# Scan of a two-layer diffusion block: bonus values from the steps' own tiles, the merged inverse evicted where it is made, the state evicted behind the output products

## Chip, cores and metric

One Trainium2 chip, one of its cores. A core has five engines that run side by side, each through its own list of instructions in order: TensorE (PE, whose weight loads the profile lists apart as PEld), VectorE (DVE), ScalarE (ACT), GpSimd (POOL) and SyncE (SP). Data comes from device memory by DMAs, which SP issues in its order, and POOL for the fill's inputs. The metric is the device time of one execution in microseconds (us), as the median of some runs; lower is better.

## What is computed

Layer 0 mixes tokens with a recurrence, layer 1 with long convolutions, and behind each stands a dense MLP. The change concerns the recurrence of layer 0 and its readout. The sequence has 256 latent tokens and 256 context tokens, 2048 channels, 32 heads of 64.

```python
def step(S, inp):
    w_t, k_t, v_t, kk_t, b_t = inp[:5]
    S = (S * w_t[:, :, None, :]
         - jnp.einsum('bhvk,bhk->bhv', S, kk_t)[..., None] * b_t[:, :, None, :]
         + v_t[..., None] * k_t[:, :, None, :])
    out = jnp.einsum('bhvk,bhk->bhv', S, inp[5]) if emit else None
    return S, out
...
S_f, oc_f = wkv_scan(S0, rc, decc[0], kdc[0], vc, kkc, bc[0], False)
S_b, oc_b = wkv_scan(S0, rc, decc[1], kdc[1], vc, kkc, bc[1], True)
_, o_f = wkv_scan(S_f, r, dec[0], kd[0], v, kk, b[0], False)
_, o_b = wkv_scan(S_b, r, dec[1], kd[1], v, kk, b[1], True)
...
# readout of o = o_f + o_b: GroupNorm by head, bonus, gate, projection
o = ((o - mean) * lax.rsqrt(var + LNX_EPS)).reshape(B, L, D) * lnx_w + lnx_b
bonus = jnp.sum(r[None] * kd * r_k, axis=(0, -1))[..., None] * v
g = jax.nn.sigmoid((h + xx * mu[5]) @ g1) @ g2
return ((o + bonus.reshape(B, L, D)).astype(h.dtype) * g) @ w_o
```

Each direction is scanned over the context first, for its state alone, and from that state over the latent tokens, with outputs.

## The kernel before

**Chunks and groups.** The recurrence is not run token by token. Tokens are taken in chunks of 64, and within a chunk everything becomes products of 64x64 matrices: a triangular system is inverted once, and a step then makes four kinds of products with its inverse, the values and the state. The 32 heads are done in eight groups of four: two pairs of heads (`pi`), each pair on 128 partitions with one head to each half of 64 (`hs`). Both directions (`d`) run at once. A group has eight steps (`i`): steps 0 to 3 are the four context chunks (`st` 0), steps 4 to 7 the four latent chunks (`st` 1, with outputs).

**One step** (`scan_step`) has three parts, between which other work is put, so that PE has something to do while another engine evicts what it made:

- j=0: products of the values `VU` with `N` and of the decayed inputs with the state `Z`, into the PSUM tile `pr`; ACT evicts the sum to `rhs`.
- j=1: products of the inverse `Y` (tile yf in the profile) with `rhs`, into the other half of `pr`, and of the state with the decay, into the first writes of `po`; ACT evicts the former, negated, to the half of `VU` that holds no values. In a step with outputs, products of the state with the queries too.
- j=2: products of `KR` with the whole of `VU` give the new state, in half 1 of `po`; ACT evicts it as `Z`. In a step with outputs, products of `VU` with `KR` (sc<-KR,VU in the profile) add to half 0 of `po`, and ACT or DVE put them into `OT`. Both halves of `po` lie in one PSUM bank.

**What is put between.** `rwkv_scan` writes the order out by hand. In each third n = 3 i + j of a step it emits, in this order: the step's own part; at j=0 the matrices of the next step (`scan_products`: three PSUM tiles of the pool sg, evicted as NT and KR); at j=1 the loads of the next step's values (`scan_values`, four DMAs); so many pieces of the next group's preparation as `SCHED[n]` says; at j=1 one piece of the modulation's product (`ada`); in the thirds of `READ` one piece of the previous group's readout; and at j=1 and j=2 three pieces of a fill: the projection of the values of the next group (`fill_v`) or of the queries of the one behind it (`fill_r`), 18 products of 128x256 a time (fl in the profile), whose inputs fx POOL loads into three buffers. In the eighth group there is nothing to prepare, and the filters of layer 1 take the fill's place.

While `self.pins` is set, each instruction of PE, ACT and DVE depends on the one before it on its engine, so that the scheduler keeps this order. DMAs are free.

**The pool sg** has three buffers of one bank, taken in turn by `scan_products`, the preparation's products, the readout's and the modulation's transposes. A product that takes a buffer waits until what was in it is evicted.

**Preparation** of a group (`scan_prepare`, 36 pieces): the decays, `KB` and `ard`; the matrices `Mn`; `scan_bonus`, which sums r*k*r_k over a head's channels and leaves the sum `bs` of a pair, 128x256, in SBUF; then 31 steps of substitution on DVE (tmp and d in the profile), which invert blocks of 32; two transposes on DVE; and the merge of the blocks: two product groups with `Mn` (sg<-d,Mn, line 1207), evicted to `G`, and one group with `G` (sg<-d,d, line 1221), made in the last third of the group. Its result `py` is evicted to `Y` by four copies of 32 partitions, two on DVE and two on ACT, a piece of its own (lines 1223 to 1226). `prep` carries this piece over: it is taken in the first third of the next group, ahead of `scan_products` (line 919).

**Readout** (`scan_readout`, lines 1293 to 1354) of a group runs in the thirds `READ` = 6, 7, 9 (first pair) and 13, 14, 16 (second pair) of the next group. In the first third it loads the gate `gt`, takes the mean and squares; in the second it takes the variance, scales by lnx_w, and then loads the latent values of the pair again (`values`, two DMAs of 64 KB in rows of 256 B, into the tile sqo that the squares have left); in the last third PE transposes the values by products with the identity (sg<-ident,sqo), DVE multiplies them by `bs`, adds, multiplies by the gate, and SP stores y. The last group's readout (`late`) does its loads in step 5, the rest at the end, both pairs side by side.

**Values** lie in device memory as `v` (group, 512 tokens, 256), with the columns of a group ordered pair, head, channel, so a chunk's load for one head of both pairs has rows of two times 64 numbers (256 B each).

Of the kernel before, what the change touches and what calls it, by code (L numbers as in the profile page):

```python
# [18 lines left out]
P = 128  # L19
# [49 lines left out]
class Kern:  # L69
# [802 lines left out]
    def rwkv_scan(self, es, prep_pools, ngroups=KT // 2):  # L872
# [88 lines left out]
    def scan_values(self, g, i):  # L961
# [12 lines left out]
    SCHED = (1, 1, 1, 2, 1, 2, 1, 1, 2, 1, 1, 2, 1, 2, 2, 1, 2, 2, 1, 2, 2, 1, 2, 1)  # L974
# [134 lines left out]
    def scan_bonus(self, pi, res):  # L1109
# [41 lines left out]
    def scan_prepare(self, g):  # L1151
# [70 lines left out]
        yield  # L1222
# [5 lines left out]
    def scan_step(self, g, i):  # L1228
# [12 lines left out]
        for pi, d, blk, c in blks:  # L1241
            for h, hp in enumerate(hs):
                self.product(pr[hp, 0, blk, :], N[hp, blk, :], VU[hp, pi, d, h, :], start=True, stop=not i)
# [22 lines left out]
        nc.scalar.mul(VU[hs[1], :, :, 0, :], v4(pr[hs[1], 1]), -1.0)  # L1266
        nc.scalar.mul(VU[hs[0], :, :, 1, :], v4(pr[hs[0], 1]), -1.0)
# [25 lines left out]
    def scan_readout(self, g):  # L1293
# [8 lines left out]
        src = scr["v"][g, L:, :].rearrange("(c s) (p h v) -> h s c p v", s=64, h=2, v=64)  # L1302

        def pair(pi):
            m = 2 * g + pi
            tile_ = lambda: (self.sc if last and pi else self.sg).tile([P, 512], F32, name="sc" if last and pi else "sg")
            gt = rp.tile([P, L], F32, name="gt", bufs=n)
            nc.sync.dma_start(gt, scr["gate"][m * P : (m + 1) * P, :])
            o = OT[:, pi, :]
            bs = res["bs", pi]  # L1310

            def values():
                V = rp.tile([P, L], F32, name="sqo", bufs=n)[:].rearrange("p (c v) -> p c v", v=64)
                for h in range(2):
                    nc.sync.dma_start(V[64 * h : 64 * h + 64], src[h][:, :, pi, :])
                yield
                pt = self.sg.tile([P, 512], F32, name="sg")
                for c in range(4):
                    for hp in self.HS:
                        self.product(pt[hp, c * 64 : c * 64 + 64], V[hp, c, :], self.ident[hp, hp], start=True, stop=True)  # L1320
                nc.vector.tensor_tensor(bs, pt[:, :L], bs, op=ALU.mult)

            if last:
                yield from values()
                yield
# [11 lines left out]
            if last:  # L1337
                yield
            else:
                yield from values()  # L1340
# [5 lines left out]
        if last:  # L1346
            its = [pair(0), pair(1)]
            for _ in range(5):
# [374 lines left out]
def layout(inp):  # L1723
# [11 lines left out]
        "w_r": g["rw_w_r"], "w_k": g["rw_w_k"], "w_v": g["rw_w_v"], "w_o": g["rw_w_o"],  # L1735
# [41 lines left out]
```

## Time and profile before

| | us |
|---|---|
| median of 3 runs | 3775.41 (3771.19 to 3782.73) |
| profiled execution | 3769.96 |
| its span | 3768.1 |
| the scan within it, from the first step to the last output | about 580 to 1516 |
| mean granted TensorE clock | 0.944 |
| busy: PE, DVE, ACT, POOL | 3402.8, 2513.1, 1741.7, 684.7 |

The profile gives times of one execution, on its one core. In its rows "a<-b,c" means that a tile named a is written from b and c; a line number is often a helper's (L110 is `product`, L53 the wrapper of ACT and DVE), so groups are told apart by tile names. "Idle before" is the time in which the engine stood still ahead of an instruction, and behind the arrow stands what ended it. [...] The names of two operands come in no fixed order. fp32 products are carried out as several instructions, so counts are multiples of those in the code.

### The profile page before, as it was taken

What the parts mean: (1) busy time and instruction counts of PE and PEld (TensorE: products, weight loads), DVE (VectorE), ACT (ScalarE), POOL (GpSimd) and SP (SyncE); (2) the same over time, 40 slices, a digit from 0 to 9 for tenths busy, and PEclk for the clock granted to TensorE, in tenths of its full rate; (3) what the DMA queues carried; (4) which work ended last, traced back from release to release, by engine and by line L of the source; (5) the groups of instructions that cost most, each with busy time, mean ns of one, the idle gap of its engine ahead of it and who ended that gap; (6) DMA issues with size and microseconds to landing.
All of it is one profiled execution on the core that took longest, in us unless ns stands there. A gap on an engine that the chain in (4) does not pass through costs nothing.

```text
span 3768.1 us, 82300 instructions
## 1 busy us (share of the span) xinstructions
PE 3402.8 (90%) x34206; PEld 3119.8 (83%) x34206; DVE 2513.1 (67%) x3857; ACT 1741.7 (46%) x3045; POOL 684.7 (18%) x706
## 2 busy tenths in 40 slices
PE   7798888888888879889999999899998899999997
PEld 3376677777777767889999999899998799999997
DVE  5887676556566665578776776677787674646554
ACT  4444444443344434444343435465665663534342
POOL 2632221111111100110000001524443730000003
PEclk9899999888888979999999999999999999999998
DMA  9678798887788754668888887566665675656553
GB/s 322 192 229 262 247 314 260 236 237 224 220 236 238 232 149 131 208 207 292 265 276 268 281 266 238 168 216 218 214 218 173 218 232 182 187 182 186 183 184 108
DMA packets 694367, 838.34 MB, mean 222 GB/s; under 512 B 81055, under 2 KB 562240, under 8 KB 693992
## 3 DMA queue, kind: packets, MB, share of 16 engines
q1 hardware_dynamic: 662888, 719.82, 61.1%
q0 software_dynamic: 31104, 113.26, 9.8%
q8 instruction: 268, 4.39, 0.5%
q14 instruction: 107, 0.88, 0.1%
HBM read 778.36 MB, written 54.59 MB: 221 GB/s over the span
## 4 chain that ended last, share of the span: by engine, by line
PE 43%; DMA 15%; DVE 10%; issue 9%; ACT 4%; POOL 3%; SPq 1%; POOLq 0%; ACTq 0%; DVEq 0%
PE mm L158 11%; PE mm L159 11%; PE mm L160 11%; DMA aw<-in_ada_w 7%; PE fl L110 3%; DMA w<-in_mlp_up 2%; DVE wl L53 2%; PE sg L110 2%; PE sc L110 2%; POOL acc L293 2%; DMA sqo<-v 2%; DVE acc L53 1%; DMA fx<-xv 1%; ACT wh L53 1%; ACT aw L53 1%
## 5 line engine op out<-in xcount | busy, mean ns | idle before, releaser
L53 DVE TENSOR_TENSOR wl<-w,wh 128x1024 fp32r<-128x1024 f32 (+1 forms) x716 | 925.4, 1296 | 552.9 <-ACT wh L53 542.4
L53 ACT CAST wh<-w 128x1024 fp32r<-128x1024 f32 (+1 forms) x716 | 741.4, 1044 | 775.7 <-PE mm L159 479.3
L158 PE MATMUL mm<-hxh,wh 128*128 128x258 f32 (+1 forms) x3072 | 873.2, 286 | 23.3 <-ACT hxh L53 18.1
L160 PE MATMUL mm<-hxh,wl 128*128 128x258 f32 (+1 forms) x3072 | 870.7, 285 | 8.7 <-DVE wl L53 8.6
L159 PE MATMUL mm<-hxl,wh 128*128 128x258 f32 (+1 forms) x3072 | 872.1, 284 | 0.2 <-DVE hxl L53 0.2
L158 PEld LDWEIGHTS mm<-hxh,wh 128*128 128x128 f32 x3072 | 582.6, 190 | 26.8 <-ACT hxh L53 19.0
L160 PEld LDWEIGHTS mm<-hxh,wl 128*128 128x128 f32 x3072 | 581.7, 190 | 13.2 <-DVE wl L53 11.6
L159 PEld LDWEIGHTS mm<-hxl,wh 128*128 128x128 f32 x3072 | 584.3, 190 | 3.2 <-DVE hxl L53 1.3
L159 PE MATMUL mm<-ul,wh 128*128 128x256 f32 x2048 | 579.2, 283 | 8.0 <-DVE ul L53 7.8
L158 PE MATMUL mm<-uh,wh 128*128 128x256 f32 x2048 | 578.4, 283 | 5.5 <-ACT uh L53 5.5
L160 PE MATMUL mm<-uh,wl 128*128 128x256 f32 x2048 | 577.9, 282 | 0.0
L293 POOL TENSOR_TENSOR acc<-acc,aw 128x512 f32<-128x512 f32 x180 | 276.5, 1536 | 895.0 <-ACT aw L53 853.1
L159 PEld LDWEIGHTS mm<-ul,wh 128*128 128x128 f32 x2048 | 391.2, 191 | 9.1 <-DVE ul L53 9.1
L158 PEld LDWEIGHTS mm<-uh,wh 128*128 128x128 f32 x2048 | 391.0, 191 | 6.0 <-ACT uh L53 5.9
L160 PEld LDWEIGHTS mm<-uh,wl 128*128 128x128 f32 x2048 | 391.6, 191 | 0.0
L53 DVE SCALAR_TENSOR_TENSOR acc<-aw,sc,acc 128x512 f32<-128x512 f32 x300 | 230.9, 770 | 105.9 <-DMA aw<-in_ada_w 103.3
L110 PE MATMUL fl<-fh,fx 128*128 128x256 f32 x1024 | 233.7, 315 | 21.7 <-DMA fx<-xv 19.9
L110 PEld LDWEIGHTS fl<-fh,fx 128*128 128x128 f32 x1024 | 184.9, 212 | 43.2 <-DMA fx<-xv 24.9
L53 ACT ACTIVATE aw<-aw,sc 128x512 f32<-128x512 f32 x180 | 126.1, 719 | 134.3 <-DMA aw<-in_ada_w 126.8
L53 DVE TENSOR_TENSOR flo<-fr,fh 128x512 fp32r<-128x512 f32 x128 | 87.7, 686 | 124.8 <-ACT fh L53 120.5
L751 POOL DMA_DIRECT2D fx<-xv x128 | 67.9, 530 | 534.4 <-PE fl L110 520.4
L110 PE MATMUL sg<-ard,KB 64*64 64x64 f32 (+1 forms) x3584 | 135.0, 249 | 32.9 <-ACT yf L53 26.0
(351 smaller groups left out, 6203.9 us busy)
## 6 DMA issues: line engine op xcount, KB each, us to landing
aw<-in_ada_w SPq DMA_DIRECT2D x288, 512.0 KB, 5.9
w<-in_mlp_down SPq DMA_DIRECT2D x128, 1024.0 KB, 5.5
w<-in_mlp_up SPq DMA_DIRECT2D x120, 1024.0 KB, 6.3
fx<-xv POOLq DMA_DIRECT2D x128, 512.0 KB, 6.3
aw<-in_ada_w SPq DMA_DIRECT2D x192, 256.0 KB, 3.0
w<-in_hy_in_w SPq DMA_DIRECT2D x44, 1024.0 KB, 5.8
fx<-xr POOLq DMA_DIRECT2D x64, 512.0 KB, 5.5
w<-in_w_k SPq DMA_DIRECT2D x16, 1024.0 KB, 7.8
```

Source lines behind the costliest of these rows:

```text
L53: return self.kern.pin(self.key, f(*a, **kw))
L110: return self.pin("pe", self.nc.tensor.matmul(out, lhsT=lhsT, rhs=rhs, **kw))
L158: nc.tensor.matmul(out, lhsT=wh, rhs=xh, start=first, stop=False)
L159: nc.tensor.matmul(out, lhsT=wh, rhs=xl, start=False, stop=False)
L160: nc.tensor.matmul(out, lhsT=wl, rhs=xh, start=False, stop=last)
L293: nc.gpsimd.tensor_tensor(acc, acc, w[:, a], op=ALU.add)
L751: self.nc.gpsimd.dma_start(x, src)
```

## The change

- `scan_prepare` loses the piece between the inverse's last products and its eviction; both are one piece now, the 35th, in the last third of the group. `prep` carries nothing over. `SCHED` has the same sum, with its entries for thirds 21, 22 and 23 changed from 1, 2, 1 to 2, 1, 1.
- The values' columns are ordered group, head, pair, channel: the host permutes the columns of `w_v`, and `VU` is laid out [direction, head, pair, 64]. A load of a chunk for one head takes rows of 128 numbers (512 B).
- The bonus is multiplied in the steps with outputs: at j=1, behind the state's products with the queries, four products with the identity transpose the values that `VU` holds for that chunk into a tile of sg, and DVE multiplies them into `bs`, which is one tile for both pairs.
- In a step with outputs the products into half 0 of `po` come ahead of the eviction of `Z`, not behind it.
- The readout loads no values. The gate is loaded in the second third, behind the scaling by lnx_w, into the tile sqo that the squares have left. In the last group the readout has three rounds, all at the end, and nothing in step 5.

```diff
-        prep = iter((None,))
...
-            prep = itertools.chain(prep, () if last else self.scan_prepare(g + 1))
+            prep = iter(()) if last else self.scan_prepare(g + 1)
...
-                take(prep, 1)
                 prep_pools.close()
...
-                            take(prep, i == 0 and not last)
                             for _ in nxt:
                                 pass
...
-                if i == 5 and last:
-                    pins, self.pins = self.pins, None
-                    take(late, 1)
-                    self.pins = pins
...
-            src = self.scr["v"][g, t0 : t0 + 64, :].rearrange("s (p h v) -> h s p v", h=2, v=64)
             for h, hp in enumerate(self.HS):
-                self.nc.sync.dma_start(VU[hp, :, d, h, :], src[h])
+                self.nc.sync.dma_start(VU[hp, d, h], self.scr["v"][g, t0 : t0 + 64, h * P : (h + 1) * P].rearrange("s (p v) -> s p v", v=64))
...
-    SCHED = (1, 1, 1, 2, 1, 2, 1, 1, 2, 1, 1, 2, 1, 2, 2, 1, 2, 2, 1, 2, 2, 1, 2, 1)
+    SCHED = (1, 1, 1, 2, 1, 2, 1, 1, 2, 1, 1, 2, 1, 2, 2, 1, 2, 2, 1, 2, 2, 2, 1, 1)
...
-        bs = self.ge.tile([P, L], F32, name="bs", bufs=5)
-        self.nc.scalar.copy(bs, pb[:, :L])
-        res["bs", pi] = bs
+        if not pi:
+            res["bs"] = self.ge.tile([P, 2, L], F32, name="bs", bufs=3)
+        self.nc.scalar.copy(res["bs"][:, pi, :], pb[:, :L])
...
-        yield
         for d in range(2):
             for h in range(2):
                 (nc.scalar.copy if h else nc.vector.tensor_copy)(Y[part(h, d), d, :, 32 - 32 * d : 64 - 32 * d], py[part(h, d)])
...
+            pt = self.sg.tile([P, 2, 64], F32, name="sg")
+            for pi in range(2):
+                for h, hp in enumerate(hs):
+                    self.product(pt[hp, pi, :], VU[hp, 0, h, pi, :], self.ident[hp, hp], start=True, stop=True)
+            bs = res["bs"][:, :, 64 * il : 64 * il + 64]
+            nc.vector.tensor_tensor(bs, bs, pt, op=ALU.mult)
         yield
         if i < 7:
             for pi, d, blk, c in blks:
                 for h in range(2):
-                    mm(h, 1, blk, KR[:, h, blk, 0, :], VU[:, pi, d, h, :])
+                    mm(h, 1, blk, KR[:, h, blk, 0, :], VU[:, d, h, pi, :])
+        if st == 1:
+            for pi, d, blk, c in blks:
+                for h in range(2):
+                    mm(h, 0, blk, VU[:, d, h, pi, :], KR[:, h, blk, 1, :])
+        if i < 7:
             Zn = cp.tile([P, 4, 64], F32, name="Z")
             nc.scalar.copy(Zn, po[:, 1])
             res["Z"] = Zn
         if st == 1:
-            for pi, d, blk, c in blks:
-                for h in range(2):
-                    mm(h, 0, blk, VU[:, pi, d, h, :], KR[:, h, blk, 1, :])
...
-            gt = rp.tile([P, L], F32, name="gt", bufs=n)
-            nc.sync.dma_start(gt, scr["gate"][m * P : (m + 1) * P, :])
...
-            def values():
-                V = rp.tile([P, L], F32, name="sqo", bufs=n)[:].rearrange("p (c v) -> p c v", v=64)
-                for h in range(2):
-                    nc.sync.dma_start(V[64 * h : 64 * h + 64], src[h][:, :, pi, :])
-                yield
...
-            if last:
-                yield
-            else:
-                yield from values()
+            gt = rp.tile([P, L], F32, name="sqo", bufs=n)
+            nc.sync.dma_start(gt, scr["gate"][m * P : (m + 1) * P, :])
+            yield
             nc.vector.scalar_tensor_tensor(dv, dv, self.col("lnx_b", m), bs, op0=ALU.add, op1=ALU.add)
             nc.vector.tensor_tensor(dv, dv, gt, op=ALU.mult)
             nc.sync.dma_start(scr["y"][m * P : (m + 1) * P, :], dv)
...
+        "w_v": g["rw_w_v"].reshape(1, D, 8, 2, 2, 64).swapaxes(3, 4).reshape(1, D, D), "w_o": g["rw_w_o"],
```

More of the change, by code (lines that the diff above doesn't have):

```diff
@@ L1242, in scan_step @@
             for h, hp in enumerate(hs):
-                self.product(pr[hp, 0, blk, :], N[hp, blk, :], VU[hp, pi, d, h, :], start=True, stop=not i)
+                self.product(pr[hp, 0, blk, :], N[hp, blk, :], VU[hp, d, h, pi, :], start=True, stop=not i)
             if i:
@@ L1265, in scan_step @@
         v4 = lambda t: t.rearrange("p (a d) v -> p a d v", d=2)
-        nc.scalar.mul(VU[hs[1], :, :, 0, :], v4(pr[hs[1], 1]), -1.0)
-        nc.scalar.mul(VU[hs[0], :, :, 1, :], v4(pr[hs[0], 1]), -1.0)
+        for h in range(2):
+            nc.scalar.mul(VU[hs[1 - h], :, h].rearrange("p d a v -> p a d v"), v4(pr[hs[1 - h], 1]), -1.0)
         if st == 1:
@@ L1275, in scan_step @@
                 for h in range(2):
-                    mm(h, 1, blk, KR[:, h, blk, 0, :], VU[:, pi, d, h, :])
+                    mm(h, 1, blk, KR[:, h, blk, 0, :], VU[:, d, h, pi, :])
+        if st == 1:
+            for pi, d, blk, c in blks:
+                for h in range(2):
+                    mm(h, 0, blk, VU[:, d, h, pi, :], KR[:, h, blk, 1, :])
+        if i < 7:
             Zn = cp.tile([P, 4, 64], F32, name="Z")
@@ L1301, in scan_readout @@
         rp = self.rp if last else gp
-        src = scr["v"][g, L:, :].rearrange("(c s) (p h v) -> h s c p v", s=64, h=2, v=64)
         def pair(pi):
@@ L1306, in pair @@
             tile_ = lambda: (self.sc if last and pi else self.sg).tile([P, 512], F32, name="sc" if last and pi else "sg")
-            gt = rp.tile([P, L], F32, name="gt", bufs=n)
-            nc.sync.dma_start(gt, scr["gate"][m * P : (m + 1) * P, :])
             o = OT[:, pi, :]
-            bs = res["bs", pi]
-            def values():
-                V = rp.tile([P, L], F32, name="sqo", bufs=n)[:].rearrange("p (c v) -> p c v", v=64)
-                for h in range(2):
-                    nc.sync.dma_start(V[64 * h : 64 * h + 64], src[h][:, :, pi, :])
-                yield
[L1317 to L1321, printed above, removed]
-            if last:
-                yield from values()
-                yield
+            bs = res["bs"][:, pi, :]
             ps = tile_()
@@ L1336, in pair @@
             nc.vector.scalar_tensor_tensor(dv, dv, self.col("lnx_w", m), sq, op0=ALU.mult, op1=ALU.mult)
-            if last:
-                yield
-            else:
-                yield from values()
+            gt = rp.tile([P, L], F32, name="sqo", bufs=n)
+            nc.sync.dma_start(gt, scr["gate"][m * P : (m + 1) * P, :])
+            yield
             nc.vector.scalar_tensor_tensor(dv, dv, self.col("lnx_b", m), bs, op0=ALU.add, op1=ALU.add)
@@ L1347, in scan_readout @@
             its = [pair(0), pair(1)]
-            for _ in range(5):
+            for _ in range(3):
                 for it in its:
@@ L1734, in layout @@
         "ada_w": g["ada_w"], "mlp_up": g["mlp_up"], "mlp_down": g["mlp_down"],
-        "w_r": g["rw_w_r"], "w_k": g["rw_w_k"], "w_v": g["rw_w_v"], "w_o": g["rw_w_o"],
+        "w_r": g["rw_w_r"], "w_k": g["rw_w_k"],
+        "w_v": g["rw_w_v"].reshape(1, D, 8, 2, 2, 64).swapaxes(3, 4).reshape(1, D, D), "w_o": g["rw_w_o"],
         "dec_w1": g["rw_dec_w1"], "dec_w2": g["rw_dec_w2"], "a_w1": g["rw_a1"], "a_w2": g["rw_a2"],
```

## The prediction

> **What bounds the kernel now.** The change touches the scan alone, from 580 to 1516 us of the span, so after the page's head I read the scan: its windows, PE's groups and waits there, and single stretches of the timeline.
>
> ```profile
> span 3768.1 us, 82300 instructions
> ```
>
> The windows of the scan (us; busy time of PE, PEld, DVE, ACT, POOL; granted clock, DMA share, GB/s), one of the eight groups of four heads, then the first seven together:
>
> ```profile
> 813.00:930.00 117.00, 97.79 (x1884) 86.48 (x1884) 72.05 (x154) 50.29 (x120) 13.85 (x27) 0.88 0.81 233
> 580.00:1380.00 800.00, 667.90 (x13079) 588.88 (x13078) 497.18 (x1065) 345.05 (x823) 90.68 (x171) 0.88 0.79 231
> ```
>
> A group takes about 117 us. PE is the busiest engine, yet idles 800 - 668 = 132 us of the 800, and its clock is 0.88. Both can be gained. Who ends PE's idle time, in groups of instructions (busy us, mean ns, idle before) and as waits (total, times, longest):
>
> ```profile
> L110 PE MATMUL fl<-fh,fx 128*128 128x256 f32 x896 | 204.3, 315 | 12.2 <-DMA fx<-xv 12.2
> L110 PE MATMUL sg<-ard,KB 64*64 64x64 f32 (+1 forms) x3184 | 117.5, 249 | 32.2 <-ACT yf L53 26.0 <-DVE NT L53 3.7 <-ACT KR L53 2.5
> L110 PE MATMUL sc<-KR,VU 128*64 128x64 f32 x448 | 20.4, 237 | 18.9 <-ACT Z L53 18.9
> L110 PE MATMUL sg<-d,Mn 32*32 32x32 f32 x896 | 19.1, 203 | 10.3 <-issue 8.1 <-DVE d L53 2.1
> L110 PE MATMUL sg<-ident,sqo 64*64 64x64 f32 x192 | 15.3, 291 | 40.1 <-DMA sqo<-v 31.8 <-DVE d L53 5.6 <-DVE tmp L53 2.8
> ```
>
> ```profile
> PE sg L110 <- DMA sqo<-v: 31.8, 15, 6.4
> PE sg L110 <- ACT yf L53: 26.0, 7, 4.2
> PE sc L110 <- ACT Z L53: 18.9, 21, 2.3
> ```
>
> PE waits 40.1 us for the readout's values, 26.0 for the merged inverse's eviction (3.7 a group) and 18.9 for the state's eviction: 85 of the 132 us, and the change goes at these three.
>
> **What a wait costs beyond itself** is seen in the clock, microsecond by microsecond (PE busy, clock, DMA share, GB/s), behind a wait for values:
>
> ```profile
> 846.00:847.00 1.00, 0.70 (x24) 1.00 1.19 319
> 847.00:848.00 1.00, 0.00 (x0) 1.00 1.21 259
> 848.00:849.00 1.00, 0.00 (x0) 0.68 1.10 243
> 849.00:850.00 1.00, 0.00 (x0) 0.50 0.73 182
> 850.00:851.00 1.00, 0.94 (x16) 0.50 0.14 40
> ...
> 855.00:856.00 1.00, 1.00 (x9) 0.91 0.35 71
> ```
>
> The clock halves while PE idles, some 2 us after its last product (846.7 to 848.7), and stays at 0.50 for 6.8 us (0.64 + 6 + 0.18). What that costs the fill's products:
>
> ```profile
> 882.60 0.41 PE L110 MATMUL fl<-flo,fx 128*128 128x256 f32 x1
> 882.81 0.63 PE L110 MATMUL fl<-fh,fx 128*128 128x256 f32 x2
> ...
> 888.26 0.28 PE L110 MATMUL fl<-fx,flo 128*128 128x256 f32 x1
> 888.38 0.40 PE L110 MATMUL fl<-fx,fh 128*128 128x256 f32 x2
> ```
>
> From one product's start to the next it is 0.21 us at half clock and 0.12 at full: 43% is lost. A clock of 0.88 over 800 us is 2 x 0.12 x 800 = 192 us at half, some 28 stretches of 6.8. In microsecond windows I count 17 of them right behind one of the first two waits (last below); PE is busy for some 5.7 us of a stretch, so one costs 2.5 us, and the 17 cost 43.
>
> ```profile
> 1312.00:1313.00 1.00, 0.00 (x0) 0.00 (x0) 0.00 (x0) 0.58 (x2) 0.00 (x0) 0.79 0.52 171
> ```
>
> Here the clock fell after 2 us without a product, so value waits of 31.8 / 15 = 2.1 us in the mean count too. [...]
>
> **The change, part by part.**
>
> **Bonus values in the steps.** Gone are the loads sqo<-v, the transposing products behind them and their wait: 40.1 us. The same 16 transposes a group now run as four bursts of four, reading tiles already loaded: no difference on PE. On DVE two products of 128x256 become four of 128x128.
>
> ```profile
> L53 DVE TENSOR_TENSOR bs<-sg,bs x16: 416/425/426, 731.4 to 1506.7; 128x256 f32<-128x256 f32 x16
> ```
>
> ```profile
> L53 DVE TENSOR_TENSOR OT<-OT,sc x32: 277/280/289, 662.4 to 1504.5; 128x128 f32<-128x128 f32 x32
> ```
>
> That is 4 x 0.28 - 2 x 0.425 = +0.3 us a group, on an engine that has 45 us of a group to spare. The burst adds a wait: it takes one of the three sg buffers, which only DVE's multiplication gives back, and the state's products and all fills stand behind it on PE. Nothing of before shows it; bounds are 0 and the 3.7 us that the inverse's eviction costs. Nearest is the wait for DVE's NT, behind like products: 3.7 us in seven groups, 0.5 each. I take 0.3.
>
> **The gate's load** moves behind the scaling by lnx_w, where the value loads stood on SP, so SP waits there as now, one load instead of three; its queue loses the early gate load and both value loads of each readout. Behind it wait only DVE's product with the gate and the store of y; before, DVE stood there for PE anyway. Its landing (3.1 us against 5.9, below) should come first.
>
> **Merged inverse evicted at once.** Four copies move from the next group's first phase to the last phase of this one:
>
> ```profile
> 917.97 0.67 DVE L53 COPY yf<-sg 32x512 f32<-32x512 f32 x1
> ...
> 920.06 0.58 ACT L53 COPY yf<-sg 32x512 f32<-32x512 f32 x1 [0.75 <-DVE yf L53]
> ```
>
> ```profile
> 911.72 2.12 PE L110 MATMUL sg<-d,d 32*32 32x32 f32 x128
> ...
> 920.69 1.44 PE L110 MATMUL sg<-ard,KB 64*64 64x64 f32 x34 [3.77 <-ACT yf L53]
> ```
>
> DVE and ACT take turns, each waiting for the other (first and last of four shown): a chain of 2.7 us. Started at 914.1, behind the inverse's last product (913.8), they end at 916.8; PE has other work until 920.69 - 3.77 = 916.9 anyway. About 0.5 us of 3.7 stays: 7 x 3.2 = 22 us gained. The fill's eviction and cast stand behind them on ACT, the cast's remainder on DVE, up to 0.6 us later, with a fill's length to spare. SCHED moves the inverse's first product group one phase forward; there it needs the sg buffer that NT's eviction frees, 0.5 us a group: -4, while the 8.1 us of "issue" behind its dense products may shrink (0 taken).
>
> **State behind the output products.** PE no longer waits 18.9 us. The state comes later by the output products, 20.4 / 28 steps = 0.7 us, but a fill of 18 products (18 x 0.12 = 2.1 us) runs before it is read: I take 17.
>
> [...]
>
> **Rows of 512 B.**
>
> ```profile
> q1 hardware_dynamic: 662888, 719.82, 61.1%
> ```
>
> ```profile
> VU<-v SPq DMA_DIRECT2D x256, 32.0 KB, 5.0
> gt<-gate SPq DMA_DIRECT2D x16, 128.0 KB, 3.1
> sqo<-v SPq DMA_DIRECT2D x32, 64.0 KB, 5.9
> ```
>
> VU's 32,768 packets of 256 B become half as many; the 8,192 of sqo go. A packet of this queue takes 0.611 x 16 x 3768 / 662888 = 56 ns in the mean (1,086 B), so 24,576 fewer are worth at most 85 us of the scan's DMA time, and by bytes (2 MB) 2 us. DMA is not the bound: I take 0.
>
> **The end of the scan** pays once. The last readout's early call in step 5 goes with the loads that it issued; its gate load now starts behind DVE's first product, where it lay ready.
>
> ```profile
> 1512.75 0.88 DVE L53 SCALAR_TENSOR_TENSOR dv<-dv,cols,sqo 128x256 f32<-128x256 f32 x2 [0.84 <-ACT sqo L53]
> ...
> 1514.34 0.76 DVE L53 TENSOR_TENSOR dv<-dv,gt 128x256 f32<-128x256 f32 x2
> ```
>
> 1512.75 + 0.44 + 3.1 = 1516.3 instead of 1514.3, less the transposes gone from there: +1 us, between 0 and +4.
>
> **Sum.** Idle: 40 + 22 + 17 - 4 - 10 (32 bursts at 0.3) - 1 = 64 us. Clock: 17 x 2.5 = 43. Together 107, or 15 a group. Not all will stay: DMA works 0.80 x 117 = 94 us of a group (0.79 and 0.81 above), so at 102 us its share would be 0.92, fills would wait longer for fx, and DVE, which is full in places, comes to set the pace there:
>
> ```profile
> 863.00:873.00 10.00, 8.81 (x116) 7.74 (x112) 9.15 (x27) 3.39 (x10) 1.14 (x3) 1.00 0.72 207
> ```
>
> I let a quarter come back, 27 us: **-80 us**. The profiled execution took 3770 us (span 3768.1 and 1.9 around it), 5.4 under the median of 3775.4; so 3690 against it, 3695 against the median. I give 3693.
>
> **Rivals.** *All of it stays* and the DMAs keep up: 107, with the 10 of the bursts and the 8 of issue back 125: 3650. For it: DMA falls idle behind each wait (0.14 above). Against: shares over 1 ahead of it. *The wait moves on:* fx and DVE take two thirds, 107 / 3 = 36 us stay: 3739. For it: the DVE row. [...] *Slower:* the sg buffers. If DVE is so late that each burst holds its buffer until PE's next products need it, PE waits in 32 steps. At the inverse's 3.7 us with a stretch of half clock behind (2.5) that is 198 us against 117 gained: 3856. It decides from 117 / 32 = 3.7 us a step on, the clock's loss counted. For it: 9.15 of 10 us above; against: DVE's multiplication stands ahead of its long substitution work in each phase.
>
> **Numbers.** Forecast 0.45, all stays 0.16, wait moves on 0.20, only long waits 0.08, doesn't do it 0.05, slower 0.06. The first four are faster by over 0.3% (11 us, about what a measurement of this kernel tells from no change): 0.89; within 0.05; slower 0.06. From 3635 to 3750 lie the forecast with its open prices, the fourth, and most of the second and the third.
>
> **What would show it.** Right: no sqo<-v; idle before sg<-ard,KB under 10 us and before sc<-KR,VU under 3; clock 0.93 or more from 580 on; groups of 104 to 107 us. Wrong: groups under 100 us (nothing came back); fl waiting over 40 us for fx, or PE for DVE's flo, d and tmp (the wait moved); idle of over 2 us before the bursts or the KR products with DVE as releaser (slower).

## The result, and the profile after

| | median us | ratio to before, 95% interval |
|---|---|---|
| before | 3773.66 (3771.19 to 3782.73, 4 runs) | |
| after | 3717.39 (3705.65 to 3719.61, 4 runs) | 0.984 [0.9814, 0.9867] |

The change makes the kernel 56 us faster; 3693 was forecast, in a range of 3635 to 3750. The profiled execution of the changed kernel took 3705.65 us. Its page and its windows, in the same columns as before (one whole group, the first seven groups, and what follows the scan):

```profile
span 3703.6 us, 82273 instructions
```

```profile
893.00:996.00 103.00, 88.96 (x1860) 78.40 (x1861) 69.67 (x153) 48.69 (x118) 13.33 (x26) 0.93 0.85 256
574.10:1296.10 722.00, 628.50 (x13105) 555.30 (x13105) 495.31 (x1077) 340.07 (x817) 90.68 (x171) 0.93 0.84 251
1446.00:3703.00 2257.00, 2134.68 (x17112) 2099.78 (x17112) 1519.90 (x2007) 1067.51 (x1621) 408.38 (x358) 0.97 0.68 215
```

The group shown takes 103 us, the one that the prediction showed 117; in the mean of the first seven it is 103.1 against 113.5. Cut at the same events (first product of the values to the first product of the filters, which ends the seventh group), the seven groups of before are this row:

```profile
581.00:1375.60 794.60, 665.80 (x13073) 587.82 (x13072) 495.09 (x1061) 342.32 (x816) 90.68 (x171) 0.88 0.79 230
```

So 73 us are gained in the seven groups: 35 of PE's idle time (794.6 - 665.8 = 128.8, now 722.0 - 628.5 = 93.5) and 37 of its busy time, which is the clock, 0.93 for 0.88 with nearly the same products. Outside them, this one execution was 7 us shorter ahead of the scan than that of before and 15 us longer behind the seven groups. Of the 15, 7 lie in the eighth group up to the last store of y (147.6 us against 140.2) and 8 behind it. From that store on, the profiled executions of this study take between 2245 and 2260 us whatever the kernel, so the sum over the program scatters by some 15 us, and the seven groups are what to read.

PE's groups, from 573 to 1293 us (busy us, mean ns, idle before and what ended it; the durations overlap: of the fill's products that the prediction lists, the one at 882.60 lasts 0.41 us, and the next starts 0.21 us behind its start):

```profile
L110 PE MATMUL fl<-fh,fx 128*128 128x256 f32 x896 | 185.2, 295 | 5.6 <-DMA fx<-xv 5.5
L110 PE MATMUL sg<-ard,KB 64*64 64x64 f32 (+1 forms) x3144 | 114.1, 245 | 41.0 <-ACT KR L53 36.8 <-DVE NT L53 3.7
L110 PE MATMUL sc<-Z,ard 64*64 64x64 f32 x1456 | 79.1, 226 | 7.0 <-ACT Z L53 6.9
L110 PE MATMUL sg<-d,Mn 32*32 32x32 f32 x896 | 20.2, 204 | 10.2 <-issue 5.0 <-ACT KR L53 2.9 <-DVE d L53 2.2
L110 PE MATMUL sc<-KR,VU 128*64 128x64 f32 x448 | 19.4, 233 | 0.0
L110 PE MATMUL sg<-ident,VU 64*64 64x64 f32 x224 | 12.3, 228 | 4.2 <-DVE NT L53 2.9 <-issue 1.3
```

The three waits at which the change goes are gone under their old names: no sg<-ident,sqo (40.1), the output products sc<-KR,VU wait 0.0 (18.9), and the inverse's eviction yf no longer stands ahead of sg<-ard,KB (26.0) in six of its seven places. The seventh is at the start of the eighth group, just behind this window: there PE still waits 5.1 us for yf, because two of the copies stand on ACT and the last of them behind a cast that waits for its load. But that same group of products idles more than before, 41.0 against 32.2 us: **ACT KR** took the place of yf. That is a new wait, and the experiments are about it.

**Where the new wait stands.** At the start of each group from the second on, in its second step, PE stands still for 6.2 to 8.2 us. Five of these six waits are named KR; that of the second group is named Z (6.2 us ahead of sc<-Z,ard) and stands behind another load on ACT. The third group (timeline, then PE busy, clock, DMA share, GB/s by the microsecond):

```profile
794.66 1.10 PE L110 MATMUL sg<-ard,KB 64*64 64x64 f32 x46
803.01 0.48 PE L110 MATMUL sg<-ard,KB 64*64 64x64 f32 x4 [7.25 <-ACT KR L53]
```

```profile
797.00:798.00 1.00, 0.00 (x0) 1.00 1.15 391
798.00:799.00 1.00, 0.00 (x0) 0.59 1.12 357
...
808.00:809.00 1.00, 1.00 (x10) 0.79 0.50 166
```

The clock halves again, about 2.4 us after the last product (795.8). Followed back, on ACT and then on DVE:

```profile
790.95 0.62 ACT L53 CAST fh<-fr 128x512 fp32r<-128x512 f32 x1 [1.20 <-DMA fr<-in_w_v]
...
801.67 0.62 ACT L53 CAST fh<-fr 128x512 fp32r<-128x512 f32 x1 [8.53 <-DMA fr<-in_w_v]
802.32 0.37 ACT L53 COPY rhs<-sc 128x256 f32<-128x256 f32 x1
802.58 0.66 ACT L53 COPY KR<-sg 128x256 f32<-128x256 f32 x2
```

```profile
776.20 0.47 DVE L53 SCALAR_TENSOR_TENSOR rb<-kx,cols,rb 128x256 f32<-128x256 f32 x1
...
792.53 0.48 DVE L53 SCALAR_TENSOR_TENSOR rb<-kx,cols,rb 128x256 f32<-128x256 f32 x1 [5.00 <-DMA rb<-ri]
...
794.74 0.69 DVE L53 TENSOR_TENSOR flo<-fr,fh 128x512 fp32r<-128x512 f32 x1
```

KR's eviction has nothing to wait for but its turn: ahead of it on ACT stands the cast fh of the fill's weights, and that waits 8.53 us for a load. The load could start only when DVE had read the weight buffer (flo, ended 795.4; in the seven groups SP waits for flo ahead of such loads 28.9 us, 26 times), and flo stood on DVE behind an operation of the next group's preparation that waited 5.00 us for its own load, rb. (The chain of waits names the landing of a modulation load, 11.3 us after its issue, at the same 795.44 as what released the weight load; the two can't be told apart by time, but see the runs that move those loads.) This is only a part of the 8.53 us: flo also needed its own cast, which ended at 791.57, so the wait for rb can have put it off by at most 794.74 - 791.57 = 3.2 us. The load itself then took some 6 us from its issue at 795.50, where such loads take 4.8 us in the median. ACT took its instructions here in the order in which the program pins them: rhs and KR start 0.65 and 0.91 us behind the start of a cast that they have nothing to do with.

**Why rb is late now and wasn't before.** SP's queue, after and before:

```profile
774.61 0.37 SPq L851 DMA_DIRECT2D r<-fe  x1
...
779.40 1.29 SPq L1025 DMA_DIRECT2D rx<-r  x2
...
783.48 0.60 SPq L1016 DMA_DIRECT2D rb<-ri  x1
...
795.50 0.38 SPq L778 DMA_DIRECT2D fr<-in_w_v  x1
```

```profile
800.01 0.37 SPq L851 DMA_DIRECT2D r<-fe  x1
...
806.68 0.81 SPq L1033 DMA_DIRECT2D rx<-r  x2
...
811.14 0.46 SPq L1024 DMA_DIRECT2D rb<-ri  x1
```

```profile
806.29 0.48 DVE L53 SCALAR_TENSOR_TENSOR rb<-kx,cols,rb 128x256 f32<-128x256 f32 x1
...
819.70 0.48 DVE L53 SCALAR_TENSOR_TENSOR rb<-kx,cols,rb 128x256 f32<-128x256 f32 x1
```

At a group's start the fill's last queries are stored (r<-fe), and their reload (rx<-r) stands on SP until the store has landed (23.8 us in six waits, the longest 4.7). The loads for the later pieces of the preparation stand behind it. Before, DVE's first operation of the preparation (806.29) came 6.3 us behind the issue of that store, because the two copies of yf stood ahead of it; its third came 8.6 us behind the issue of the rb load (811.14) and found the data there. After, the first comes 1.6 us behind the store (776.20 against 774.61), and the third is ready at 792.53 - 5.00 = 787.53, 4.05 us behind the issue at 783.48: too early. The reload still comes late behind the store: 4.8 us from one to the other here, 6.7 before. In all seven groups of before, the first operation comes within 1.6 us of the reload, before or after it; from the second group on it now comes 3.2 to 4.8 us ahead of it. The prompt eviction lets DVE reach a load sooner that can't start as much sooner.

### The profile page after: what moved, and what is told of

Its sections match the earlier page's. It is cut to its first block, busy times and chain, and to the rows that moved or that the text cites. A ratio compares the mean times of both kernels' runs of the same rounds, so it can differ in the third digit from the quotient of the medians.

```text
span 3703.6 us, 82273 instructions
## 1 busy us (share of the span) xinstructions
PE 3370.4 (91%) x34206; PEld 3090.5 (83%) x34206; DVE 2511.4 (68%) x3873; ACT 1739.1 (47%) x3045; POOL 683.2 (18%) x706
## 4 chain that ended last, share of the span: by engine, by line
PE 50%; DMA 20%; DVE 14%; issue 6%; ACT 5%; POOL 4%; SPq 0%; ACTq 0%; POOLq 0%; DVEq 0%
PE mm L159 11%; PE mm L158 11%; PE mm L160 11%; DMA aw<-in_ada_w 9%; PE sg L110 4%; PE fl L110 4%; PE sc L110 3%; DVE wl L53 2%; POOL acc L293 2%; DVE acc L53 2%; DMA w<-in_mlp_up 2%; DMA w<-in_mlp_down 1%; DVE xt L53 1%; DMA fr<-in_w_v 1%; DMA a<-l2t 1%
## 5 line engine op out<-in xcount | busy, mean ns | idle before, releaser
L160 PE MATMUL mm<-hxh,wl 128*128 128x258 f32 (+1 forms) x3072 | 872.6, 285 | 10.2 <-DVE wl L53 10.2
L159 PE MATMUL mm<-ul,wh 128*128 128x256 f32 x2048 | 579.7, 283 | 10.2 <-DVE ul L53 10.2
L159 PEld LDWEIGHTS mm<-ul,wh 128*128 128x128 f32 x2048 | 391.6, 191 | 11.3 <-DVE ul L53 11.3
L110 PE MATMUL fl<-fh,fx 128*128 128x256 f32 x1024 | 213.2, 296 | 9.8 <-DMA fx<-xv 8.4
L110 PEld LDWEIGHTS fl<-fh,fx 128*128 128x128 f32 x1024 | 168.4, 194 | 27.8 <-issue 13.0
L110 PEld LDWEIGHTS sg<-ard,KB 64*64 64x64 f32 x3584 | 113.6, 137 | 55.7 <-ACT KR L53 37.8
```

The source lines that it names most:

```text
L110: return self.pin("pe", self.nc.tensor.matmul(out, lhsT=lhsT, rhs=rhs, **kw))
L159: nc.tensor.matmul(out, lhsT=wh, rhs=xl, start=False, stop=False)
L160: nc.tensor.matmul(out, lhsT=wl, rhs=xh, start=False, stop=last)
```

## The experiments

Ratios are to runs of the kernel before, on the same chip in the same series; 0.3% are about 11 us. "Seven groups" are cut as above, from each profile. k0 to k3, k4 to k8 and k10 to k13 are three series on three chips, in which the kernel before took 3770.88, 3769.22 and 3773.01 us. k0, the mark, ran in the first alone, so comparisons with it across series are good to a few us only.

| run | median us | ratio, 95% interval | seven groups, us | PE idle in them |
|---|---|---|---|---|
| before (profile) | 3773.66 | | 794.6 | 128.8 |
| k0_as_is | 3705.32 | 0.9818 [0.9798, 0.9838] | 721.4 | 95.8 |
| k1_state_first | 3710.47 | 0.984 [0.9816, 0.9864] | 729.5 | 101.6 |
| k2_inverse_deferred | 3702.43 | 0.9816 [0.9794, 0.9839] | 719.5 | 86.3 |
| k3_rows_256 | 3701.97 | 0.9825 [0.9802, 0.9847] | 735.5 | 100.5 |
| k4_values_again | 3743.22 | 0.9928 [0.9909, 0.9946] | 771.9 | 123.2 |
| k11_values_alone | 3707.75 | 0.9829 [0.9803, 0.9856] | 735.1 | 96.8 |
| k6_less_ada | 3671.42 | 0.9747 [0.9733, 0.9762] | 693.2 | 72.2 |
| k7_cast_later | 3728.01 | 0.9891 [0.9878, 0.9904] | 743.1 | 107.6 |
| k8_ada_moved | 3691.19 | 0.9788 [0.9775, 0.98] | 715.8 | 85.5 |
| k10_moved_deferred | 3693.72 | 0.9783 [0.9763, 0.9804] | 715.3 | 91.5 |
| k12_before_moved | 3759.28 | 0.9962 [0.9945, 0.9978] | 783.0 | 134.4 |
| k13_ada_middle | 3683.95 | 0.9765 [0.9742, 0.9787] | 713.3 | 83.3 |

### One part undone at a time

The changed kernel once more, as the mark for the others:

> The changed kernel once more, as the measure for its neighbours on one chip: 3717 us, ratio to before 0.985.

It took 3705.32 us, at the fast end of its first series (3705.65 to 3719.61). Differences under some 10 us between these runs say nothing.

The state's eviction put back ahead of the output products:

```
+        if i < 7:
+            Zn = cp.tile([P, 4, 64], F32, name="Z")
+            nc.scalar.copy(Zn, po[:, 1])
+            res["Z"] = Zn
         if st == 1:
             for pi, d, blk, c in blks:
                 for h in range(2):
                     mm(h, 0, blk, VU[:, d, h, pi, :], KR[:, h, blk, 1, :])
-        if i < 7:
-            Zn = cp.tile([P, 4, 64], F32, name="Z")
-            nc.scalar.copy(Zn, po[:, 1])
-            res["Z"] = Zn
```

> The state evicted ahead of the output products again, all else as changed. Theory (each wait that PE loses in the middle of a group is gained in full): PE waits some 17 us before sc<-KR,VU again and the time rises by 12 to 20 us over the changed kernel's. Rival (the wait only stands elsewhere, as the stretch of a group is set by its loads): within 5 us of the changed kernel.

```profile
PE sg L110 <- ACT KR L53: 36.0, 14, 7.0
PE sc L110 <- ACT Z L53: 19.3, 22, 2.7
```

In PE's waits (total, times, longest) the state's wait is back in full, 19.3 us. The time is 3710 us: 5 more than the mark, with intervals that overlap. Of the 17 us that the order was to bring, at most a third can be seen. PE's idle time in the seven groups is 6 us more than the mark's, as KR (36.0 for 40.6) and flo (4.5 for 9.0) give way.

The inverse evicted in the next group again, with the old `SCHED`:

```
-            prep = iter(()) if last else self.scan_prepare(g + 1)
+            prep = itertools.chain(prep, () if last else self.scan_prepare(g + 1))
...
+                            take(prep, i == 0 and not last)
...
+        yield
         for d in range(2):
             for h in range(2):
                 (nc.scalar.copy if h else nc.vector.tensor_copy)(Y[part(h, d), d, :, 32 - 32 * d : 64 - 32 * d], py[part(h, d)])
```

> The merged inverse evicted in the next group's first phase again, with the old SCHED, all else as changed. Theory (the start of a group is now set by its loads, and the cast of the fill's weights on ACT waits there for 5 to 8 us a group anyway): the eviction's 3.7 us hide in that wait, and the time is within 12 us of the changed kernel's. Rival (the prediction's term): 22 us of idle time and 18 of clock come back, 3757 us.

```profile
PE sg L110 <- ACT yf L53: 22.4, 6, 4.1
...
PE sg L110 <- ACT KR L53: 2.8, 7, 0.7
```

The same time, 3702 us, with the waits exchanged: yf comes back and KR falls to 2.8. DVE no longer waits for rb at all. This shows the new wait to be the other side of the old one: the 22 us of the inverse are not in the kernel's time, in either order. Nearly every run has the exchange. Where the inverse is evicted late (before, k2, k10, k11, k12) PE waits 26 to 30 us for yf in the seven groups (the 22.4 above leave the seventh wait out) and DVE at most 2.1 for rb. Where it is evicted at once (after, k0, k1, k3, k4, k6, k8, k13) DVE waits 26 to 43 us for rb, and PE 3.3 to 5.5 us for yf, once. The exception is k7, with 4.6 us for yf and only 1.7 for rb: there DVE is held up elsewhere (110.7 us for NT) and comes late to rb without the copies.

Rows of 256 B again, the weight columns in their old order:

```
-  self.nc.sync.dma_start(VU[hp, d, h], self.scr["v"][g, t0 : t0 + 64, h * P : (h + 1) * P].rearrange("s (p v) -> s p v", v=64))
+  self.nc.sync.dma_start(VU[hp, d, h], self.scr["v"][g, t0 : t0 + 64, :].rearrange("s (p h v) -> h s p v", h=2, v=64)[h])
...
-        "w_v": g["rw_w_v"].reshape(1, D, 8, 2, 2, 64).swapaxes(3, 4).reshape(1, D, D),
+        "w_v": g["rw_w_v"],
```

> The values in rows of 256 B again, all else as changed. Theory (the DMA engines are full at the start of each group, share 1.0 to 1.17, so packets count there): 5 to 15 us slower than the changed kernel. Rival (bytes count, and they are the same): within 4 us of it.

The page's count of packets, with the long rows and then with the short ones:

```profile
DMA packets 669278, 836.24 MB, mean 226 GB/s; under 512 B 39583, under 2 KB 537152, under 8 KB 668904
```

```profile
DMA packets 685663, 836.24 MB, mean 225 GB/s; under 512 B 72352, under 2 KB 553537, under 8 KB 685289
```

16,385 packets more, and 3701.97 us: nothing, against the theory. (The profiled execution, from which the 735.5 us of the table come, was the slowest of its five, 3719.34.) The loads' median landing is 4.7 and 5.0 us.

The values read again for the readout, the rest of the change kept:

```
+        src = scr["v"][g, L:, :].rearrange("(c s) (h p v) -> h s c p v", s=64, h=2, v=64)
...
+            gt = rp.tile([P, L], F32, name="gt", bufs=n)
+            nc.sync.dma_start(gt, scr["gate"][m * P : (m + 1) * P, :])
+            def values():
...
+                nc.vector.tensor_tensor(bs, pt[:, :L], bs, op=ALU.mult)
...
-            pt = self.sg.tile([P, 2, 64], F32, name="sg")
-            for pi in range(2):
-                for h, hp in enumerate(hs):
-                    self.product(pt[hp, pi, :], VU[hp, 0, h, pi, :], self.ident[hp, hp], start=True, stop=True)
-            bs = res["bs"][:, :, 64 * il : 64 * il + 64]
-            nc.vector.tensor_tensor(bs, bs, pt, op=ALU.mult)
```

> The values read again and transposed in the readout, the gate loaded first, all else as changed (inverse evicted at once, state behind the outputs, rows of 512 B). Theory (the bonus values carry the gain, since undoing any other part costs under 6 us): at least 45 of the 65 us come back, 3750 us or more. Rival (the loads set the length of a group, whichever wait is taken away): within 20 us of the changed kernel's 3705.

```profile
PE sg L110 <- ACT KR L53: 34.6, 13, 6.3
PE sg L110 <- DMA sqo<-v: 21.9, 18, 2.6
```

3743.22 us: 38 of the 65 us are given back, less than the theory said and more than the rival. With the wait for values in place, the other parts bring 3769.22 - 3743.22 = 26 us; the next run shows that without it they bring nothing.

### The values alone

The kernel before with the bonus values from the steps' tiles, and nothing else but the gate's load and the last readout that go with them: the changed kernel with the edits of k1, k2 and k3 together.

> The kernel before with only the bonus values taken from the steps' tiles: state, inverse and rows as before. Theory (the values' wait and its clock carry the gain; the waits for the inverse and the state only change places): 3700 to 3720, as the whole change; the wait for the inverse's eviction (yf) back at 15 to 26 us, the wait for KR small. Rival (each of the three waits carries its own share of the gain): undoing inverse and state costs 30 us or more: 3735 to 3750.

```profile
L110 PE MATMUL sg<-ard,KB 64*64 64x64 f32 (+1 forms) x3184 | 115.8, 247 | 32.9 <-ACT yf L53 26.3 <-DVE NT L53 3.7 <-ACT KR L53 2.6
L110 PE MATMUL sc<-KR,VU 128*64 128x64 f32 x448 | 19.9, 234 | 15.4 <-ACT Z L53 15.4
```

```profile
579.60:1314.70 735.10, 638.33 (x13104) 564.66 (x13104) 492.14 (x1077) 342.09 (x817) 90.69 (x171) 0.92 0.84 248
```

3707.75 us, as fast as the whole change (3705 and 3717 in its two series), though PE waits 26.3 us for yf and 15.4 for Z as it did before. The theory holds: one part of four carries the gain. Its seven groups are 13 us longer than those of the whole change (735.1 and 722.0 in one execution each); its whole time shows nothing of that.

### What stands behind the new wait

Three quarters of the modulation's weights in the scan are left unread here (each load brings the first 128 of its 512 rows, which are used four times), so that DMA has less to move:

```
-            nc.sync.dma_start(w, self.I["ada_w"][layer, k4 * 512 : (k4 + 1) * 512, c0 : c0 + 256].rearrange("(a p) n -> p a n", p=P))
+            nc.sync.dma_start(w[:, 0], self.I["ada_w"][layer, k4 * 512 : k4 * 512 + P, c0 : c0 + 256])
```

> As changed, but the modulation's loads in the scan fetch a quarter of their weights (and its products use that quarter four times): the modulation from the scan is not the reference's. Theory (full DMA engines make the loads late at a group's start): the waits there, 6 to 8 us in five groups with their half clock, vanish, and the time falls by 35 to 60 us, to 3645 to 3670. Rival (the order of ACT's and SP's instructions makes them late): within 12 us of the changed kernel's 3705.

```profile
PE sg L110 <- ACT KR L53: 21.1, 13, 5.5
```

```profile
DVE rb L53 <- DMA rb<-ri: 43.0, 6, 7.7
```

34 us faster than the mark, 3671.42, with KR down to 21.1 and a clock of 0.96 in the seven groups. So the bytes cost time, just under the least that the theory said; but the waits at a group's start did not vanish as it had said. DVE waits longer for rb than ever, 43.0 us, although the DMA share fell from 0.84 to 0.77: that wait does not come of full DMA engines alone, which fits the reading of SP's queue above.

The cast of the fill's weights called only at j=1, so that it does not stand ahead of KR:

```
-                        self.feed_hi()
+                        if j == 1:
+                            self.feed_hi()
```

> As changed, but the cast of the fill's weights on ACT is emitted in the first two thirds of a step alone, so none stands ahead of a step's rhs and KR. Theory (the weights land late for lack of DMA): PE then waits at the fill for them, and the time stays within 8 us of the changed kernel's 3705. Rival (the cast's place in ACT's order is the cause): the waits on KR, 37 us with the clock behind them, go, and the time falls by 20 us or more.

```profile
PE fl L110 <- DVE flo L53: 44.9, 31, 2.4
PE sg L110 <- ACT sqo L53: 15.9, 9, 5.9
```

KR's wait goes (4.5 us), and the kernel becomes 23 us slower, 3728: the fill now waits for its weights. Neither expectation came true: moving the cast did free KR, and it cost time elsewhere. The cast's place ahead of KR was the better of the two.

The eight modulation loads of a group moved out of its first two steps, as many in all:

```
-                        take(ada, 1)
+                        take(ada, (0, 0, 1, 1, 1, 1, 2, 2)[i])
```

> As changed, but the modulation's pieces are taken in steps 2 to 7 (two each in 6 and 7) and none in steps 0 and 1 of a group, so that their loads of 512 KB leave the full stretch at its start for its end, where the DMA share is 0.44 to 0.72. Theory (DMA): 10 to 30 us faster than the changed kernel's 3705. Rival (order): within 5 us.

```profile
DVE rb L53 <- DMA rb<-ri: 37.3, 6, 8.1
```

```profile
PE sg L110 <- ACT KR L53: 16.8, 13, 6.3
```

14 us faster than the mark by the medians, KR at 16.8. The wait for rb stays (37.3): the modulation's loads are not what holds it. They are a large part of what held KR, which falls by more than half while the wait for rb does not.

Both together, the loads moved and the inverse evicted late:

> The eight loads of modulation weights moved within the group as in the run before it that moved them, and the inverse evicted in the next group again. Theory (late loads at a group's start hide what the prompt eviction is worth; with the loads relieved it shows): the eviction's wait of 3.2 us in seven groups stands alone again, 3705 to 3715, against 3691 with the prompt eviction. Rival (the load wait at a group's start still covers it, or another wait takes its place): 3685 to 3697.

```profile
PE sg L110 <- ACT yf L53: 27.2, 7, 4.6
```

3693.72 against 3691.19: no difference again. My theory fell: it took the modulation's loads for those that hide what the prompt eviction is worth. They aren't; with yf's wait at 27.2 us DVE waits only 2.1 us for rb, so the exchange is the same as in k2.

The loads moved in the kernel before:

> The kernel before with only the loads of modulation weights moved within the group. Theory (a group's start was set by the eviction's chain there, and full DMA engines came to set it only once groups were 103 us long): little to gain, 3762 to 3775. Rival (the DMA engines were full at a group's start already and cost the kernel before as much): 14 us less as in the changed kernel, 3755 to 3760 or lower.

3759.28, 14 us less (8 to 21 by the interval), as in the changed kernel: inside the rival's range, and 3 us outside the theory's. What crowding these loads cause, or most of it, was there before the change.

None of them in the first and the last step of a group:

```
+                        take(ada, (0, 1, 1, 1, 1, 2, 2, 0)[i])
```

> The changed kernel with the eight loads of modulation weights a group at steps 1 to 6, two at steps 5 and 6 and none at steps 0 and 7, so that the DMA engines are freer both ahead of a group's start and behind it. Theory (rb and fr land late because those loads stand beside them there): faster than the first distribution with its two loads at step 7, 3670 to 3688; wait for KR under 17 us. Rival (any distribution does the same, the bytes of a group set it): 3688 to 3705.

3683.95 us, 0.9765 [0.9742, 0.9787], the fastest of the kernels that do all the work, 21 us under the mark; its lead over k8 lies within the intervals. KR is down to 4.0 us, yet DVE's wait for rb is still 36.2, and PE's idle time in the seven groups is 83.3 us, hardly less than in k8 (85.5): other waits came (for DVE mod 10.4, ACT rhs 8.4, ACT fh 5.5). The three longest for mod, 2.1 to 3.3 us, end 2.4 us behind DVE's wait for rb: that wait reaches PE by another way here. (The profiled executions of k8 and k13 were the slowest of their runs.)

A third buffer for the fill's weights wasn't tried. Nor was the edit that the reading of SP's queue asks for: the reload rx behind the preparation's other loads. That the prompt eviction would then pay is argued from the timeline and from the exchange of waits, not shown. How much of KR's wait comes of rb, and how much of the late landing of the weights themselves, was not separated.

## Why the prediction was right, and where it failed

The direction, the range and the likeliest case were right; the size was 24 us too large by the first series (3717 for 3693), 12 by the second. Step by step:

- **Bonus values: the mechanism right, with its clock.** The forecast had 40 us of idle time and, for the ten of 17 stretches of half clock that stand behind value waits, 10 x 2.5 = 25 us: 65. The part alone gives 3773.01 - 3707.75 = 65 us. That the numbers are equal is partly luck. The terms -10 for the bursts and -1 for the end belong to this part too, so its forecast was 54, ahead of the quarter. And in the seven groups it gives 794.6 - 735.1 = 59.5 us: 32.0 of PE's idle time and 27.5 of its busy time. 32 is about what the loads ended (31.8 of the 40.1); the other 8 us of that row, which waited for DVE's substitution, seem not to have been gained. In windows of a microsecond I count 28 stretches in the seven groups before, 15 with the values alone, 12 after; PE is busy in 147, 90 and 59 us of them, and half of 147 - 90 is 28, the clock's part. (A stretch that begins in the last 20 us of the cut and runs into the eighth group, in all three, is left out of these counts.)
- **The inverse: the step that failed.** "7 x 3.2 = 22 us gained", and the seven stretches of half clock behind its waits, 7 x 2.5, 17 more. The copies do run behind the inverse's products with other work on PE, as worked out. But the step asked only who waits for the copies, not what else they had held back: they had kept DVE from the preparation until its loads were there. The time came back at the same place: evicted late, PE waits 26.2 us for yf (k2); evicted at once, 40.6 us for KR (k0); its idle time in the seven groups is 86 and 96 us. In the group followed above, the way back leads over DVE's wait for rb and ACT's for the weights to KR, but rb explains at most 3.2 of 8.53 us there, and k13 has rb's wait in full (36.2 us) with KR at 4.0. So that the part gives nothing is shown, and which wait takes its place depends on the order; why PE's idle time stays nearly the same stays open. The runs put the part at -3 us undone (k2) and +3 (k10): nothing. Of its seven stretches of half clock, at most three went (15 with the values alone, 12 now).
- **The state: mechanism right, its worth not.** PE's wait of 18.9 us went to 0.0. The 6.9 us at sc<-Z,ard are not its successor: 6.2 of them are the one wait at the second group's start, and in k2 this wait is 0.4. So the fill covers the later state. But undone it costs 5 us, not 17. Something else waits then; which one in each step wasn't located.
- **The terms of -4 and -10** were too careful. The burst's wait is 4.2 us in the 28 steps with it, not 10, and part of that is issue; sg<-d,Mn idles 10.2 us as before (10.3), so neither the 4 nor the return of the 8 came. The multiplication takes 0.28 us on DVE, as estimated.
- **Rows: 0, and 0 measured.** (For the 2 MB less, the prediction's own 56 ns for 1,086 B make 7 us over 16 engines, not the 2 that it gives; the forecast used neither.)
- **The end of the scan** (+1, at most +4) may have been too small: the eighth group up to the last store of y takes 140.2 us before, 143.6 in k12 and 140.1 in k4, which loads the values again, and 144.1 to 148.9 in all the others. It wasn't traced.
- **The gate's load** didn't become a wait of PE; DVE stands 6.1 us for it in the seven groups.

```profile
L53 DVE TENSOR_TENSOR dv<-dv,sqo 128x256 f32<-128x256 f32 x12 | 5.1, 425 | 6.4 <-DMA sqo<-gate 6.1
```

- **The quarter that comes back** was too little and named wrongly. 107 us were worked out, and 56 came in the first series and 65 in the second: at least 42 are missing, which is the inverse (22 - 4 + 17) and some of the state. They did not go to fx (12.2 us before, 5.5 now) or to a DVE that is full, but to waits in one place of each group, where DVE is not full but idle. The DMA share came to 0.85, where 0.92 was feared. That the forecast came as near as it did is luck in this: a quarter put by for other causes covered 27 of the missing us.
- **The rivals.** "The wait moves on" was half right: it did, to another place than it named. The 0.08 for "only long waits" is not borne out: removing value waits of 2.1 us in the mean took 27.5 us off PE's busy time in the seven groups, with the inverse's waits still there. "Slower" needed 3.7 us a step at the bursts; 4.2 us came in all.
- Of the signs named: no sqo<-v, sc<-KR,VU under 3, the clock at 0.93: right. Under 10 us before sg<-ard,KB: wrong (41.0), and that is the line that shows the failed step. Groups of 104 to 107: 103, just under. (The 117 us of the prediction were one group; its own 800 / 7 gives 114.)

## What to carry to other kernels

Before removing a wait, ask not only who waits for it but what it delays: an engine that gets to its next load sooner may gain nothing if that load hangs on a store, a queue or a buffer that doesn't move with it. Parts of a change that free the same stretch of time don't add up; here one part alone gave as much as all four, and the other three gave 26 us only while it was missing. Watch the sum of idle time rather than the names in it: without the value loads it lay between 83 and 102 us in every order of the full work but one, whichever wait stood in front.

## What the runs showed of the hardware

The half clock comes in whole pieces in these traces. Twelve stretches in the changed kernel's seven groups last 3.4, 6.8 or 10.2 us (3, 6 and 3 of them): one, two or three times 3.4. A thirteenth begins at 1276.0 and lasts 44.4 us, 13 times 3.4, into the eighth group, where PE stands still for 5.1 and 7.1 us. The wait ahead of a fall can be shorter than any of these pieces: here PE stood still for 2.1 us (PE busy, clock, DMA share, GB/s), and the clock fell, 1.7 us after work had begun again:

```profile
866.00:867.00 1.00, 0.05 (x3) 1.00 0.45 153
867.00:868.00 1.00, 0.00 (x0) 1.00 0.16 45
868.00:869.00 1.00, 0.84 (x49) 1.00 0.00 0
869.00:870.00 1.00, 1.00 (x18) 0.93 0.66 194
870.00:871.00 1.00, 1.00 (x6) 0.50 0.38 101
```

What a fall goes with is seen when the time is cut on one grid. Its step is the thirteenth part of that last stretch, 44.37 / 13 = 3.413 us, and it runs from 579.72 on, the first fall. Each of the 210 slices of this grid between 573 and 1290 us has one clock, 1.00 or 0.50; in the kernel before a grid with the same step fits as well. In these two traces, each slice at full clock in which PE was busy under 49% of the time is followed by one at half clock, and none over 67% is; between these bounds both occur. These are counts from two executions; what makes the clock fall was not shown. The slices around the wait above, the second of them with PE busy for 1.69 us of 3.41:

```profile
863.03:866.44 3.41, 2.70 (x119) 1.00 0.98 322
866.44:869.85 3.41, 1.69 (x59) 1.00 0.26 75
869.85:873.27 3.42, 3.42 (x18) 0.50 0.60 185
```

This also sets the prediction's reading right: the clock did not follow "some 2 us after" a last product, but fell 1.7 us (848.36) and 1.3 us (1312.58) after it there, and 2.4 us after it in the changed kernel (798.18), each time at the end of a slice of its grid. So here a short wait cost clock too, and more of it fell on work than behind the longer ones: the wait of 2.1 us was followed by 3.4 us of half clock, all of them with PE busy, and the six waits of 6.2 to 8.2 us by 6.8 or 10.2 us, with PE busy in 2.9 to 6.4 of them, as part of the wait lies in them. In sum, PE is busy in 59 of its 82 us at half clock, with the values alone in 90 of 96.
